# Scores of two attention branches issued in turn on two 64-row halves of the matrix array, with masks gathered behind them and more warm-up products

## The chip, the cores and the metric

The kernel runs on one core of a Trainium2 chip. The metric is device time in microseconds (us), the median of three runs. The engines that matter here are TensorE (PE for its products, PEld for the loads of its stationary operands), VectorE (DVE), ScalarE (ACT) and the queue of SyncE (SP), which issues the transfers of weights. TensorE's array has 128 rows; a product whose operands lie in 64 partitions uses one half of the rows. Products are collected in eight banks of an accumulator memory.

## The reference

Two layers of a decoder trunk on 256 tokens of 1024 channels. In each layer four token mixers read one projection of the normalised residual:

```
o_A = RG-LRU (conv4, gated linear recurrence)      o_B = GLU, causal conv31, RMSNorm, swish
o_C = (softmax1 - lambda * softmax2) V             4 heads, each with two maps of 64 query channels
o_D = softmax over the 64 keys that an indexer picks per query
      logits = relu(einsum("bqhd,bkd->bqhk", qi, ki))   8 index heads of 32 channels, one shared key
      score  = einsum("bqhk,bqh->bqk", logits, wi);  masked causally, top 64
h += W_out( sum_j sigmoid(xn W_g[j]) * (o_j W_b[j]) )
h += W_down( silu(g) * v ),  [g, v] = causal_dwconv3(RMSNorm(h) W_up)
h += sigmoid(RMSNorm(h) W_pg) * RMSNorm(p W_p)
```

Everything is float32. The change touches the score maps of o_C (differential attention) and the index logits of o_D (sparse attention).

## The kernel before

The residual is kept with channels in partitions and 256 tokens along the free axis. All weights stream once from memory in 342 pieces of at most 128 x 1024 numbers (`prep_one`, lines 213 to 215): the SP queue loads a piece, ACT rounds it to a high part `hi`, DVE subtracts to get the low part `lo`. A large product then takes three passes per 128 x 128 tile (`mm3`, lines 248 to 250: high by high, high by low, low by high), each over 256 columns. Token-major projections (lines 476 to 478) do the same with 512 columns. Five raw and six split buffers form the ring of pieces, so a piece is split when TensorE has freed an older one.

The program is written out by hand in one order. The four mixers are generators ("sides") whose steps are put between the large products by `pump`, at distances set in the table `EVERY`; a scheduler then orders each engine's own instructions. So TensorE meets a stretch of large products, then one step of a side, then large products again. The steps that the change and the prediction speak of are these:

* Index scores, in `idx_mask(b)`, line 564. For each layer, each block b of 128 queries and each group g of four index heads there is one step: 2 x 2 x 2 = 8 visits in all. The query operand holds four heads of 32 channels in 128 partitions. The key operand `ikZ` has four copies of the transposed key, copy i set to zero (by `hmask`) outside head i's 32 partitions. Four products over all 128 rows give the four maps. Kw, the number of keys, is 128 for b = 0 and 256 for b = 1.
* Differential scores, in `attend(b, hp)` of `side_c`, lines 703 and 704. For each layer, block and pair of heads there is one step, again 8 visits. Map c of a head lies in partitions 64c to 64c + 63, so each score product uses one half of the rows. Each of the four maps is followed by a mask: an identity in bf16 times the causal mask, 128 columns over all 128 rows, added into the same bank. DVE takes the maxima (line 705), ACT the exponentials.
* The sparse branch's own scores (lines 625 and 626) have the same shape, a float32 score and a bf16 mask, but with 128 channels; the change leaves them alone.

A float32 product is carried out as two passes, each with its own weight load, so it shows as two instructions in the trace. The small banks ("sp", four of them) hold all side products; the large products have four others ("mm").

At the start TensorE has no operands until ACT and DVE have split the first x tiles and weights. Line 186 gives it 12 products of a constant tile (24 passes) meanwhile.

Of the kernel before, what the change touches and what calls it, by code (L numbers as in the profile page):

```python
# [13 lines left out]
AF = mybir.ActivationFunctionType  # L14
# [4 lines left out]
P = 128  # L19
# [10 lines left out]
PIECE = 1024  # L30
EARLY = 4  # feed-forward banks computed before the mean square is known
MIX = (0, 3, 2, 1)
MIX_ORDER = (("gate", MIX[0]), ("gate", MIX[1]), ("branch", MIX[0]), ("gate", MIX[2]), ("branch", MIX[1]),
             ("gate", MIX[3]), ("branch", MIX[2]), ("branch", MIX[3]))
# how far apart the steps of the side computations lie between the products: RG-LRU, conformer,
# differential attention, sparse attention, first half of the conformer's taps
EVERY = {0: 4.8, 1: 5.1, 2: 3.3, 3: 2.9, 4: 5.5}

# columns of the channel vectors
_V = {}  # L40
# [7 lines left out]

# columns of the row vectors
_R = {}  # L50
# [6 lines left out]

# columns of the shape-only constants
_C = {}
_o = 0  # L60
for _n, _w in (("ident", 128), ("nc30", 128), ("nc38", 128), ("rope_c", 64), ("rope_s", 128), ("rope_i", 32), ("hmask", 4)):
    _C[_n] = (_o, _w)
    _o += _w
# [3 lines left out]
def unit_list(l):  # L67
    """One layer's weights in the order of their use: (key, source, pieces), a piece being
    (first k-tile, k-tiles, column ranges or counts of zero columns)."""
    u = []  # L70

    def tok(key, c0, c1, src="w_in", kt=KD):
        g = PIECE // (c1 - c0)
        u.append((key, src, [(k, g, [(c0, c1)]) for k in range(0, kt, g)]))

    def chan(key, src, c0, kt=KD, g=8):
        u.append((key, src, [(k, min(g, kt - k), [(c0, c0 + P)]) for k in range(0, kt, g)]))

    def bu(n):
        chan(("bv", n), "w_in", 1024 + n * P)  # L80
        chan(("bg", n), "w_in", 1536 + n * P)

    ple_in = [(("ple_in", i), "w_ple_in", [(0, 2, [(512 * i, 512 * i + 512)])]) for i in range(2)]
    if l:
        u.append(ple_in[0])
    for n in range(4):
        bu(n)
    if not l:
        u.append(ple_in[0])
    tok(("tok", "dq"), 3584, 4096)  # L90
    tok(("tok", "dk"), 4096, 4608)
    u.append((("ik", 0), "w_in", [(0, KD, [(4608, 4648), P - 40])]))
    tok(("tok", "cq"), 2048, 2560)
    tok(("tok", "ck"), 2560, 3072)
    tok(("tok", "cv"), 3072, 3584)
    for n in range(8):
        chan(("a", n), "w_in", n * P)
    for kind, j in MIX_ORDER:
        if kind == "gate":
            for n in range(8):  # L100
                chan(("gate", j, n), ("w_gate", j), n * P)
        else:
            for n in range(0, 8, 2):
                tok(("branch", j, n), n * P, (n + 2) * P, ("w_branch", j), 4)
    u.append(ple_in[1])
    for n in range(8):
        chan(("out", n), "w_out", n * P)
    for g in range(NG):
        chan(("upg", g), "w_up", g * P)
        chan(("upv", g), "w_up", D_FF + g * P)  # L110
    for n in range(8):
        chan(("down", n), "w_down", n * P, NG)
    for n in range(8):
        chan(("pg", n), "w_ple_gate", n * P)
    return u
# [7 lines left out]
def decoder_kernel(ctx: ExitStack, tc: tile.TileContext, w_dram, x_dram, p_dram, vec_dram, row_dram, lru_dram,  # L123
# [30 lines left out]
    def score_banks(Kw):  # L154
        """Banks for four maps [P, Kw]: (maps of the bank, bank [P, maps, Kw])."""
        n = 2 * S // Kw
        return [(range(i, i + n), smbank().rearrange("p a b -> p (a b)").rearrange("p (a b) -> p a b", a=n))
                for i in range(0, 4, n)]

# [1 line left out]
    h = [cst.tile([P, 2, S], F32, name=f"h{i}", tag=f"h{i}") for i in range(4)]  # L161
# [20 lines left out]

    # the tensor engine's clock rises with activity: keep it busy until the first operands are there
    warm = smbank()
    for _ in range(12):
        T.matmul(warm[:, 0, :], ones, ones, start=True, stop=True)

# [1 line left out]
    stream = []  # L189
# [38 lines left out]

# [1 line left out]
    def split(dst, src, scale=1.0):  # L230
        """dst = (hi, lo) from src, exactly."""
        hi, lo = dst
        if scale == 1.0:
            A.activation(hi, src, AF.Copy)  # L234
            V.tensor_tensor(lo, src, hi.bitcast(F32), op=ALU.subtract)  # L235
        else:
            A.activation(hi, src, AF.Copy, scale=scale)
            V.scalar_tensor_tensor(lo, src, scale, hi.bitcast(F32), op0=ALU.mult, op1=ALU.subtract)

    def mm3(out, wl, xs, c0, first, last):  # L240
        """out += W[:, c0:c0+128].T @ x over the piece's k-tiles."""
        wh, wlo = wl
# [23 lines left out]
    def rnorm(acc, scale, bias):  # L266
        """1 / sqrt(scale * (sum over the channels) + bias) per token: with the tokens in
        partitions [P, 2], and in every partition [P, S]."""
        t = smbank()
# [12 lines left out]
    class Norm:  # L282
        """RMSNorm over all channels of [128, 2, S] pairs. xs: split x * gain, for products whose
        result is scaled by r afterwards; xn(): split x * gain * r."""

# [50 lines left out]
    def rope(t, H, W, tab, b):  # L336
        """t [128, H, W]: rotates the first W/4 columns of each head."""
        rot = W // 4
# [17 lines left out]

    # ================= layers =================
    for l in range(L):
# [11 lines left out]

# [1 line left out]
        if l == 0:  # L372
# [32 lines left out]
        if l:  # L405
            embed(0)
# [1 line left out]
        nrm = nxt_nrm  # L408
# [20 lines left out]

# [1 line left out]
        sv = st([P, 44], "sv", 2)  # L431
# [33 lines left out]
        def tok_unit(xk, n, npieces):  # L465
            """u[:, cols] token-major, one bank per token block."""
            pcs = take(npieces)
# [15 lines left out]
        def weave(gens):  # L483
            """The steps of the generators in turn."""
            live = list(gens)
            while live:
                for g in list(live):
                    if next(g, "end") == "end":
                        live.remove(g)
                    else:  # L490
                        yield
# [13 lines left out]

# [1 line left out]
        def side_d():  # L507
# [14 lines left out]
            yield  # L522
            ikZ = st([P, 4, S], "ikZ", 1)
            qT = [bt(), bt()]
# [3 lines left out]
            def idx_key(b):  # L528
# [9 lines left out]
                T.transpose(t[:, 0, :], ikr.rearrange("p h w -> p (h w)"), ident)  # L538
                for i in range(4):
                    A.activation(ikZ[:, i, bs], t[:, 0, :], AF.Copy, scale=hmask[:, i:i + 1])  # L540
# [5 lines left out]
            def idx_mask(b):  # L546
# [13 lines left out]
                for g in range(2):  # L560
                    rl = st([P, 4, S], "e4d", 2)
                    for hs, sc in score_banks(Kw):
                        for q, i in enumerate(hs):
                            T.matmul(sc[:, q, :], iqT[:, g, :], ikZ[:, i, :Kw], start=True, stop=True)  # L564
                        A.activation(rl[:, hs[0]:hs[-1] + 1, :Kw], sc, AF.Relu)
                    for i in range(4):
# [87 lines left out]

# [1 line left out]
        def side_c():  # L656
# [36 lines left out]
            def attend(b, hp):  # L693
# [5 lines left out]
                e = st([P, 4, S], "e4", 2)  # L699
                for c, (maps, sc) in enumerate(score_banks(S)):  # L700
                    cs = slice(c * 64, (c + 1) * 64)
                    for hh in range(2):
                        T.matmul(sc[:, hh, :Kw], qT[hp][cs, hh, bs], kT[hp][cs, hh, :Kw], start=True, stop=False)  # L703
                        T.matmul(sc[:, hh, bs], ident_bf, nc30_bf, start=False, stop=True)  # L704
                    V.tensor_reduce(mx[:, 2 * c:2 * c + 2], sc[:, :, :Kw], axis=AX.X, op=ALU.max)
# [58 lines left out]

# [1 line left out]
        xa, ga = [], []  # L766
# [52 lines left out]

# [1 line left out]
        ypad = st([P, 4, S + 30], "ypad", 1)  # L821
# [66 lines left out]

# [1 line left out]
        for c in range(4):  # L890
# [33 lines left out]

# [1 line left out]
        mixed = {}  # L926
# [45 lines left out]

# [1 line left out]
        _, rs = rnorm(acc[0], 4.0 / D, eps[:, 1:2])  # L974
# [84 lines left out]
def _constants():  # L1059
# [5 lines left out]
             "rope_s": _rope_rows(128), "rope_i": _rope_rows(32),  # L1065
             "hmask": (r[:, None] // 32 == np.arange(4)[None, :]).astype(np.float32)}
    for n, a in parts.items():
# [5 lines left out]
def _chan(a):  # L1073
    """[C] or [taps, C] -> [128, C/128 * taps]: channel c*128+p at partition p."""
    a = np.asarray(a)
# [53 lines left out]
```

## Time and profile before

| | |
|---|---|
| median of 3 runs | 1068.01 us (1066.74 to 1068.23) |
| span of the profiled execution, first to last instruction | 1064.7 us |
| TensorE products, busy | 1056.7 us, 99% |
| weight loads, busy | 1018.3 us, 96% |
| VectorE, busy | 874.1 us, 82% |
| ScalarE, busy | 708.1 us, 67% |
| mean share of the DMA engines in the span (queue of weights) | 49.9% |
| mean granted TensorE clock | 0.998 |

The profiled execution's own device time is not listed apart from its span; the three timed runs lie 2.0 to 3.5 us above that span, which is what surrounds the first and last instruction. In forty slices of the span TensorE shows 8 tenths in the first and the last and 9 in every other, VectorE 9 in the second to the seventh (about 27 to 187 us, the first layer's mixers). Busy time of TensorE counts a product from its issue to its end; products overlap in the pipeline, so what one costs is read from the distance between starts.

### The profile page before, as it was taken

The page shows a single profiled execution, that of the slowest core. Times are in us where ns is not written, and L with a number is a line of the kernel's source. Part 1 is how long each engine was busy: PE and PEld are TensorE (multiplying, and loading weights), DVE is VectorE, ACT ScalarE, POOL GpSimd, SP SyncE. Part 2 cuts the span into 40 slices and gives each one's busy share as a digit, 9 for nine tenths or more (in the row PEclk, how much of TensorE's full clock was granted, in tenths as well). Part 3 has the DMA queues.
Part 4 walks back from the last instruction along what each step waited for, and adds up shares of the span by engine and source line. Part 5 has one row for each costly group of instructions (what it writes and reads, how often), then busy time and mean ns, then how long its engine had stood idle before and what let it go on. Part 6 is the DMA issues. An engine that isn't in the chain of part 4 may idle for free.

```text
span 1064.7 us, 20765 instructions
## 1 busy us (share of the span) xinstructions
PE 1056.7 (99%) x8168; PEld 1018.3 (96%) x8168; DVE 874.1 (82%) x1629; ACT 708.1 (67%) x1207; POOL 0.2 (0%) x4
## 2 busy tenths in 40 slices
PE   8999999999999999999999999999999999999998
PEld 8888999899999999999998899998999999999998
DVE  7999999868888997855787899997779789877554
ACT  7876788668466766544677769876685667665442
POOL 0000000000000000000000000000000000000000
PEclk9999999999999999999999999999999999999999
DMA  8755244434555365555554643443455554655541
GB/s 299 279 188 194 100 142 166 159 131 158 190 182 175 121 237 183 179 188 194 181 187 167 214 163 120 139 171 115 165 169 185 173 181 147 221 177 176 184 161 40
DMA packets 52369, 183.60 MB, mean 172 GB/s; under 512 B 5808, under 2 KB 6320, under 8 KB 52272
## 3 DMA queue, kind: packets, MB, share of 16 engines
q1 hardware_dynamic: 51408, 181.05, 49.9%
q8 instruction: 64, 1.05, 0.4%
q10 hardware_dynamic: 864, 1.24, 0.4%
q14 instruction: 33, 0.27, 0.1%
HBM read 181.21 MB, written 1.05 MB: 171 GB/s over the span
## 4 chain that ended last, share of the span: by engine, by line
PE 98%; DVE 1%; DMA 0%; ACT 0%; issue 0%; DVEq 0%
PE mm L249 27%; PE mm L248 27%; PE mm L250 27%; PE mm L476 3%; PE mm L478 3%; PE mm L477 3%; PE sp L703 2%; PE sp L564 1%; PE sp L625 1%; PE sp L733 1%; PE sp L704 0%; PE sp L648 0%; DMA vec<-in_vec_dram 0%; PE sp L277 0%; PE sp L271 0%; PE sp L683 0%
## 5 line engine op out<-in xcount | busy, mean ns | idle before, releaser
L248 PE MATMUL mm<-b,hi 128*128 128x256 f32 x2384 | 680.5, 286 | 1.9 <-ACT hi L214 1.7
L250 PE MATMUL mm<-b,lo 128*128 128x256 f32 x2384 | 675.6, 284 | 0.2 <-DVE lo L215 0.2
L249 PE MATMUL mm<-b,hi 128*128 128x256 f32 x2384 | 675.8, 284 | 0.0
L214 ACT ACTIVATE hi<-raw 128x1024 fp32r<-128x1024 f32 (+1 forms) x343 | 357.2, 1046 | 259.0 <-PE mm L249 199.0
L215 DVE TENSOR_TENSOR lo<-raw,hi 128x1024 fp32r<-128x1024 f32 (+1 forms) x343 | 411.1, 1204 | 122.8 <-ACT hi L214 120.1
L248 PEld LDWEIGHTS mm<-b,hi 128*128 128x128 f32 x2384 | 457.4, 192 | 3.0 <-ACT hi L214 1.9
L249 PEld LDWEIGHTS mm<-b,hi 128*128 128x128 f32 x2384 | 458.0, 192 | 1.3 <-issue 0.5
L250 PEld LDWEIGHTS mm<-b,lo 128*128 128x128 f32 x2384 | 457.8, 192 | 0.4 <-DVE lo L215 0.4
L840 DVE SCALAR_TENSOR_TENSOR b<-s,vec,b 128x256 f32<-128x256 f32 x240 | 103.6, 476 | 0.0
L476 PE MATMUL mm<-hi,b 128*128 128x512 f32 x160 | 62.9, 393 | 0.0
L478 PE MATMUL mm<-hi,b 128*128 128x512 f32 x160 | 62.5, 390 | 0.0
L477 PE MATMUL mm<-lo,b 128*128 128x512 f32 x160 | 62.4, 390 | 0.0
L1009 DVE SCALAR_TENSOR_TENSOR s<-mm,vec,s 128x255 f32<-128x255 f32 (+1 forms) x144 | 59.8, 474 | 1.7 <-ACT s L1003 1.7
L234 ACT ACTIVATE b<-b 128x512 fp32r<-128x512 f32 x56 | 35.0, 628 | 28.1 <-DVE b L1013 18.4
L235 DVE TENSOR_TENSOR b<-b,b 128x512 fp32r<-128x512 f32 x56 | 38.4, 686 | 12.3 <-ACT b L234 12.3
L478 PEld LDWEIGHTS mm<-hi,b 128*128 128x128 f32 x160 | 30.0, 188 | 6.4
L476 PEld LDWEIGHTS mm<-hi,b 128*128 128x128 f32 x160 | 30.0, 188 | 6.4
L1003 ACT ACTIVATE s<-mm,vec 128x256 f32<-128x256 f32 x72 | 36.1, 551 | 0.0
L477 PEld LDWEIGHTS mm<-lo,b 128*128 128x128 f32 x160 | 30.1, 188 | 5.8
L709 ACT ACTIVATE s<-sp,s,s 128x128 f32<-128x128 f32 (+1 forms) x32 | 16.0, 507 | 12.7 <-DVE s L706 12.7
L295 ACT ACTIVATE b<-h,vec 128x256 fp32r<-128x256 f32 x48 | 21.4, 497 | 2.4 <-DVE h L1041 2.4
L296 DVE SCALAR_TENSOR_TENSOR b<-h,vec,b 128x256 fp32r<-128x256 f32 x48 | 20.8, 478 | 0.8 <-ACT b L295 0.8
(206 smaller groups left out, 792.4 us busy)
## 6 DMA issues: line engine op xcount, KB each, us to landing
raw<-in_w_dram SPq DMA_DIRECT2D x325, 512.0 KB, 3.3
raw<-in_w_dram SPq DMA_DIRECT2D x16, 384.0 KB, 2.9
h<-in_x_dram SPq DMA_DIRECT2D x4, 256.0 KB, 5.1
b<-in_lru_dram SPq DMA_DIRECT2D x4, 256.0 KB, 6.1
out_dram<-h ACTq DMA_DIRECT2D x3, 256.0 KB, 2.5
row<-in_row_dram SPq DMA_DIRECT2D x2, 336.0 KB, 5.6
raw<-in_w_dram SPq DMA_DIRECT2D x2, 256.0 KB, 5.0
b<-in_p_dram SPq DMA_DIRECT2D x2, 256.0 KB, 4.9
```

The lines of the kernel that those rows point to most:

```text
L214: A.activation(hi[:, cs], raw[:, cs], AF.Copy)
L215: last_lo[0] = V.tensor_tensor(lo[:, cs], raw[:, cs], hi[:, cs].bitcast(F32), op=ALU.subtract).ins
L235: V.tensor_tensor(lo, src, hi.bitcast(F32), op=ALU.subtract)
L248: T.matmul(out, a, xh, start=first and k == 0, stop=False)
L249: T.matmul(out, a, xl, start=False, stop=False)
L250: T.matmul(out, b, xh, start=False, stop=last and k == nk - 1)
L476: T.matmul(outs[b], xk[k][0][:, bs], wh[:, kk, :], start=k == 0, stop=False)
L477: T.matmul(outs[b], xk[k][0][:, bs], wl[:, kk, :], start=False, stop=False)
L478: T.matmul(outs[b], xk[k][1][:, bs], wh[:, kk, :], start=False, stop=k == last)
L840: V.scalar_tensor_tensor(t, ypad[:, c, d:d + S], w[:, 31 * c + d:31 * c + d + 1], t, op0=ALU.mult, op1=ALU.add)
L1003: A.activation(cf[:, 2 * q + s_, :], bank[:, s_, :], AF.Identity, scale=w[:, 3 * c + 2:3 * c + 3], bias=bb[:, c:c + 1])
L1009: V.scalar_tensor_tensor(t, bank[:, s_, :S - d], w[:, 3 * c + 2 - d:3 * c + 3 - d], t, op0=ALU.mult, op1=ALU.add)
```

## The change

Differential scores: the two banks of a step are opened together; the four score products alternate between the two halves of the rows (c = 0, c = 1, c = 0, c = 1), each half writing its own bank; then one mask product per bank covers both maps of that bank (256 columns, the mask read twice). Only the first product of a bank clears it.

Index scores: `ikZ` and `hmask` shrink from four to two copies, even and odd 32-partition strips. A product uses 64 rows, in which one of the two heads is set to zero by the copy. The four products alternate between the halves, each half with its own bank; b = 0 now takes two banks in place of one, and ACT evaluates two relus of two maps each where b = 0 had one of four.

Warm-up: 19 products in place of 12. The rest of the diff removes comments, which shifts no instruction.

```
-    for _ in range(12):
+    for _ in range(19):
         T.matmul(warm[:, 0, :], ones, ones, start=True, stop=True)
...
-            ikZ = st([P, 4, S], "ikZ", 1)
+            ikZ = st([P, 2, S], "ikZ", 1)
...
-                for i in range(4):
+                for i in range(2):
                     A.activation(ikZ[:, i, bs], t[:, 0, :], AF.Copy, scale=hmask[:, i:i + 1])
...
-                    for hs, sc in score_banks(Kw):
-                        for q, i in enumerate(hs):
-                            T.matmul(sc[:, q, :], iqT[:, g, :], ikZ[:, i, :Kw], start=True, stop=True)
-                        A.activation(rl[:, hs[0]:hs[-1] + 1, :Kw], sc, AF.Relu)
+                    halves = score_banks(S)
+                    for v in range(2):
+                        for r, (_, sc) in enumerate(halves):
+                            rs = slice(64 * r, 64 * r + 64)
+                            T.matmul(sc[:, v, :Kw], iqT[rs, g, :], ikZ[rs, v, :Kw], start=True, stop=True)
+                    for hs, sc in halves:
+                        A.activation(rl[:, hs[0]:hs[-1] + 1, :Kw], sc[:, :, :Kw], AF.Relu)
...
-                for c, (maps, sc) in enumerate(score_banks(S)):
-                    cs = slice(c * 64, (c + 1) * 64)
-                    for hh in range(2):
-                        T.matmul(sc[:, hh, :Kw], qT[hp][cs, hh, bs], kT[hp][cs, hh, :Kw], start=True, stop=False)
-                        T.matmul(sc[:, hh, bs], ident_bf, nc30_bf, start=False, stop=True)
+                halves = score_banks(S)
+                for hh in range(2):
+                    for c, (_, sc) in enumerate(halves):
+                        cs = slice(c * 64, (c + 1) * 64)
+                        T.matmul(sc[:, hh, :Kw], qT[hp][cs, hh, bs], kT[hp][cs, hh, :Kw], start=hh == 0, stop=False)
+                for c, (maps, sc) in enumerate(halves):
+                    T.matmul(sc[:, :, bs], ident_bf, nc30_bf[:, None, :].to_broadcast([P, 2, P]), start=False, stop=True)
+                for c, (maps, sc) in enumerate(halves):
                     V.tensor_reduce(mx[:, 2 * c:2 * c + 2], sc[:, :, :Kw], axis=AX.X, op=ALU.max)
```

How the order of TensorE's instructions moves in the differential scores of the first layer, first block, first pair of heads, before (`sp` are banks, `b` the transposed keys and queries, `mask_bf` the identity and the mask):

```order
L703 MATMUL sp_2003<-b_1485,b_1483 128x128
L704 LDWEIGHTS mask_bf
L704 MATMUL sp_2003<-mask_bf 128x128
L703 MATMUL sp_2003<-b_1485,b_1483 128x128
L704 LDWEIGHTS mask_bf
L704 MATMUL sp_2003<-mask_bf 128x128
L703 MATMUL sp_2004<-b_1485,b_1483 128x128
L704 LDWEIGHTS mask_bf
L704 MATMUL sp_2004<-mask_bf 128x128
L703 MATMUL sp_2004<-b_1485,b_1483 128x128
L704 LDWEIGHTS mask_bf
L704 MATMUL sp_2004<-mask_bf 128x128
```

And the same place of TensorE now, where the lines have become 707 (score) and 709 (mask):

```order
L707 MATMUL sp_2010<-b_1492,b_1490 128x128
L707 MATMUL sp_2011<-b_1492,b_1490 128x128
L707 MATMUL sp_2010<-b_1492,b_1490 128x128
L707 MATMUL sp_2011<-b_1492,b_1490 128x128
L709 LDWEIGHTS mask_bf
L709 MATMUL sp_2010<-mask_bf 128x2x128
L709 LDWEIGHTS mask_bf
L709 MATMUL sp_2011<-mask_bf 128x2x128
```

The four masks became two of twice the width and stand behind all scores; the bank, and with it the half of the rows, changes at every score.

TensorE at the index scores of the first layer, second block, first group, before (`mm` is a large product's bank, `s` the index queries and the masked keys):

```order
L249 MATMUL mm_1211<-b_647,hi_1031 128x256
L250 MATMUL mm_1211<-b_646,lo_1032 128x256
L564 MATMUL sp_1245<-s_929,s_1149 128x256 x2
L564 MATMUL sp_1246<-s_929,s_1149 128x256 x2
L248 MATMUL mm_1211<-b_625,hi_1117 128x256
```

And now, where the line is 566 and the operands of a product are 64 partitions high:

```order
L249 MATMUL mm_1216<-b_654,hi_1034 128x256
L250 MATMUL mm_1216<-b_653,lo_1035 128x256
L566 MATMUL sp_1250<-s_936,s_1152 128x256
L566 MATMUL sp_1251<-s_936,s_1152 128x256
L566 MATMUL sp_1250<-s_936,s_1152 128x256
L566 MATMUL sp_1251<-s_936,s_1152 128x256
L248 MATMUL mm_1216<-b_632,hi_1120 128x256
```

The number of products and their neighbours stay; the banks alternate, and each product now goes to a half of the rows.

## Rows read from the trace of the kernel before

**Rows 1.** The page, busy time of each engine, share of the span, instructions:

```profile
PE 1056.7 (99%) x8168; PEld 1018.3 (96%) x8168; DVE 874.1 (82%) x1629; ACT 708.1 (67%) x1207; POOL 0.2 (0%) x4
```

**Rows 2.** Waits of PE: engine, line, waited for: us, times, longest:

```profile
PE mm L248 <- ACT hi L214: 1.7, 1, 1.7
```

**Rows 3.** Waits of ACT, same columns:

```profile
ACT hi L214 <- PE mm L249: 199.0, 156, 2.2
```

**Rows 4.** Waits of DVE, same columns:

```profile
DVE s L705 <- PE sp L704: 2.7, 8, 0.5
```

**Rows 5.** Busy by window: PE, PEld, DVE, ACT, POOL (instructions); clock, DMA, GB/s:

```profile
27.00:187.00 160.00, 160.00 (x1076) 146.57 (x1075) 154.01 (x385) 125.66 (x251) 0.00 (x0) 1.00 0.52 178
```

**Rows 6.** Timeline of PE, differential scores, 128 keys: start, us, line, operation, count:

```profile
157.39 0.28 PE L249 MATMUL mm<-b,hi 128*128 128x256 f32 x1
157.51 0.28 PE L250 MATMUL mm<-b,lo 128*128 128x256 f32 x1
157.72 0.48 PE L703 MATMUL sp<-b,b 64*128 64x128 f32 x2
158.14 0.23 PE L704 MATMUL sp<-mask_bf 128*128 128x128 bf16 x1
158.29 0.49 PE L703 MATMUL sp<-b,b 64*128 64x128 f32 x2
...
159.90 0.36 PE L248 MATMUL mm<-b,hi 128*128 128x256 f32 x1
```

**Rows 7.** Timeline of PE, differential scores, 256 keys:

```profile
198.42 0.70 PE L703 MATMUL sp<-b,b 64*128 64x256 f32 x2
199.05 0.23 PE L704 MATMUL sp<-mask_bf 128*128 128x128 bf16 x1
```

**Rows 8.** Timeline of PE, sparse scores and masks over all 128 rows:

```profile
175.22 0.44 PE L625 MATMUL sp<-s,b 128*128 128x128 f32 x2
175.49 0.22 PE L626 MATMUL sp<-s,mask_bf 128*128 128x128 bf16 x1
175.55 0.44 PE L625 MATMUL sp<-s,b 128*128 128x128 f32 x2
```

**Rows 9.** Timeline of PE, index scores, 256 keys:

```profile
104.95 1.89 PE L564 MATMUL sp<-s,s 128*128 128x256 f32 x8
106.49 0.47 PE L248 MATMUL mm<-b,hi 128*128 128x256 f32 x1
106.80 0.28 PE L249 MATMUL mm<-b,hi 128*128 128x256 f32 x1
```

**Rows 10.** Timeline of PE, a transposition of 40 partitions between large products:

```profile
62.17 0.39 PE L477 MATMUL mm<-lo,b 128*128 128x512 f32 x1
62.40 0.39 PE L478 MATMUL mm<-hi,b 128*128 128x512 f32 x1
62.72 0.25 PE L907 MATMUL sp<-con,s 40*128 40x40 f32 x1
62.90 0.50 PE L476 MATMUL mm<-hi,b 128*128 128x512 f32 x1
63.23 0.40 PE L477 MATMUL mm<-lo,b 128*128 128x512 f32 x1
```

**Rows 11.** Busy by window at the start; columns as in rows 5:

```profile
1.04:5.28 4.24, 4.24 (x20) 4.24 (x21) 0.10 (x1) 1.28 (x1) 0.00 (x0) 1.00 0.73 196
5.28:8.70 3.42, 1.49 (x10) 1.09 (x10) 3.06 (x10) 3.35 (x9) 0.00 (x0) 1.00 1.04 392
8.70:12.10 3.40, 3.40 (x18) 3.40 (x18) 3.12 (x9) 3.02 (x7) 0.00 (x0) 0.50 1.04 408
```

**Rows 12.** Timelines of PE and DVE at the start:

```profile
1.04 4.96 PE L186 MATMUL sp<-ones 128*128 128x128 f32 x24 [1.04 <-DVE ones L166]
11.26 1.23 DVE L215 TENSOR_TENSOR lo<-raw,hi 128x1024 fp32r<-128x1024 f32 x1 [0.21 <-ACT hi L214]
12.90 0.28 PE L250 MATMUL mm<-b,lo 128*128 128x256 f32 x1
```

More of the change, by code (lines that the diff above doesn't have):

```diff
@@ L60 @@
 _o = 0
-for _n, _w in (("ident", 128), ("nc30", 128), ("nc38", 128), ("rope_c", 64), ("rope_s", 128), ("rope_i", 32), ("hmask", 4)):
+for _n, _w in (("ident", 128), ("nc30", 128), ("nc38", 128), ("rope_c", 64), ("rope_s", 128), ("rope_i", 32), ("hmask", 2)):
     _C[_n] = (_o, _w)
@@ L1065, in _constants @@
              "rope_s": _rope_rows(128), "rope_i": _rope_rows(32),
-             "hmask": (r[:, None] // 32 == np.arange(4)[None, :]).astype(np.float32)}
+             "hmask": (r[:, None] // 32 % 2 == np.arange(2)[None, :]).astype(np.float32)}
     for n, a in parts.items():
```

## The prediction

> **What bounds the kernel now.** I read the page first: TensorE is busy in 99% of the span [rows 1]. Busy can still mean waiting, so the waits come next. Apart from the warm-up's own start, TensorE waits once worth naming, 1.7 us for the first split weights [rows 2]; ScalarE waits 199 us in 156 pieces for TensorE to free a split buffer [rows 3], so weights lie ready before they are wanted. The end is therefore set by the sum of TensorE's slots, and a slot saved anywhere behind the start is saved at the end, as long as VectorE keeps up. The tightest place for that is the first layer's mixers, where VectorE is busy 154 of 160 us [rows 5].
>
> Then I looked at slots, by distances between starts. Large products stand 0.12 us apart (157.39, 157.51). The first score on a half of the rows starts 0.21 us behind the last one, and a map costs 0.57 to 0.58 us from score to score (157.72, 158.29) [rows 6]. At 256 keys its two passes last 0.63 us to the mask instead of 0.42 [rows 6, 7]; the difference of 0.21 is 2 x 128 more columns, so 128 columns stream in 0.105 us. A map of 128 keys is then 0.21 us of score columns and 0.06 of mask (175.49 to 175.55 in rows 8), 0.27 in all, and 0.31 us of its 0.58 is something else. The sparse branch has the same two products over all 128 rows and takes 0.33 us a map [rows 8]. What differs is the change between 64 and 128 rows, there and back. Of the 0.31, about 0.09 is emptying at entry (0.21 against 0.12), about 0.11 the load of the first weights, which nothing covers, and 0.10 emptying at exit.
>
> The Trainium skill (TensorEngine Tiling (Array Packing), Key Properties) says that a change of tiling mode, not of tile, drains TensorE. These rows agree, 0.31 us for the round trip. By the same sentence a turn from one half to the other should cost nothing, which no row here shows.
>
> **The change part by part.** *Differential scores.* Each of the 8 visits made four round trips, one for each map, and now makes one: 3 x 0.31 = 0.93 us a visit, 8 x 0.93 = 7.4 us less. The masks stream as many columns as before, 2 x 256 for 4 x 128: nothing. That counts score passes as still coming one after another, as the two of one map do.
>
> *Index scores.* These ran over all 128 rows and paid no round trip: eight passes of 256 columns took 1.54 us, and the next large product kept 0.31 instead of 0.12, in all 1.73 us or 0.216 a pass, with loads hidden [rows 9]. Eight visits now each pay one: 0.09 emptying, 0.11 first load, then 0.10 emptying and 0.10 for the next large product's load. The last two are read at a transposition of 40 partitions: it starts 0.32 us behind a product where 0.23 is usual, holds 0.18 us for what is 0.03 us of columns by the 0.105 above and a short load, and the next product keeps 0.33 for 0.23 [rows 10]. In all 0.40 us a visit, 3.2 us more. The nearest rows bound it by 0.31 and 0.40 a visit, 2.5 to 3.2; I take the upper, since a large product's load follows, not a short mask's.
>
> *Two halves at once.* No row shows a product on one half next to one on the other: a mask always lay between. The bounds: a turn of halves hides nothing, or every second pass disappears behind its neighbour. Two passes of one map share a half and stay in order, so what can overlap is the second pass of one map with the first of the next. There are three such turns in a visit. At 128 keys a pass streams 0.105 us and its load takes about as long (0.11), so if loads come one after another nothing is gained. At 256 keys a pass streams 0.21. If the other half's weights are loaded only when the last pass before has begun, as a load stands one pass ahead now, 0.105 of it overlaps: 3 x 0.105 = 0.32 us a visit, with four differential and four index visits of 256 keys 2.5 us. If they are loaded earlier, 0.21 overlaps at each turn: 0.63 us a visit, 5.0 us. If the two halves also load at the same time, 128 keys gain 0.32 us a visit as well, 2.5 us more. I take the first, 2.5 us, which asks only for what the rows already show of loads, between 0 and 7.6.
>
> The Trainium skill (TensorE: Matmul & The Clock Gate, Part 3) says that products in distinct row groups start about 4 ns apart and run side by side, 3.07 times as fast with four tiles at 512 columns. No run here shows it; by it the gain would be nearer to 5.0 or 7.6 than to 2.5. It is the second rival below.
>
> *Warm-up.* The 24 passes run from 1.04 to 6.00 us, and the first 20 take 4.24 us, 0.21 each, twice the 0.105 of the rest of the kernel: the lower level, 1.2 GHz. Then TensorE idles 1.7 us for its operands; in 5.28 to 8.70 it is busy 1.49 of 3.42 us, and behind that stretch the granted clock is 0.50 from 8.70 to 12.10 [rows 2, 11, 12]. Fourteen more passes at 0.105 end at about 7.5 us, before the first operands (7.7). With the idle gap mostly filled I expect the higher level, 2.4 GHz, to stay. But the stretch is 18 products at twice their time, 1.7 us at most, and the second weight piece limits what of it can be had: its low part is ready at 11.26 + 1.23 = 12.49 us, and TensorE uses it at 12.90 [rows 12]. So 0.4 us, and a wait for VectorE takes the place of the slow clock. Bounds: 0 and 0.4; below nothing if that new wait of about 1 us lets the clock fall once more, 1.7 us lost, which I hold unlikely since it is shorter than the gap before and lies between full stretches.
>
> *Other engines.* ScalarE loses 8 key copies and gains 4 small relus; it is 67% busy [rows 1] and ahead by the buffers it waits for: nothing. VectorE's first maximum of a differential visit now waits for both halves and the masks. In its queue behind it stand splits of weights and the conformer's taps. It waited 2.7 us in 8 such places [rows 4]; the second maximum now waits for nothing, so I cost the exchange at nothing. The cover is the weights split ahead; without it, at most the 0.9 us that the visit shrinks would be handed back once.
>
> The sum against the span of 1064.7 us: -7.4 + 3.2 - 2.5 - 0.4 = -7.1, a span of 1057.6. The median of the runs lies 3.3 us above that span; carried along, 1068.0 - 7.1 = 1060.9 us.
>
> **The rivals.** *The halves do not overlap.* Scores merely stand one after another, and index scores only lose: -7.4 + 3.2 - 0.4 = -4.6, 1063.4 us. For it: nothing in the trace has ever overlapped two products' columns. Against: the halves hold separate weights and banks.
>
> *They overlap fully.* At 256 keys -9.6, 1058.4 us; with loads side by side as well -12.1, 1055.9 us. For it: nothing shared is visible in the rows but the order of issue; against: loads have always stood one pass ahead.
>
> *A turn between halves empties the array.* Then each of three turns a visit costs 0.09 to empty and 0.11 for an uncovered load, 0.20. Differential visits save only 3 x (0.31 - 0.20) = 0.33, 2.6 us in all; index visits pay 0.40 + 0.60 = 1.0, 8.0 us: -2.6 + 8.0 - 0.4 = +5.0, 1073.0 us, slower. It decides from a turn price x of 0.10: 24 x (0.31 - x) and 0.4 are gained and 3.2 + 24x lost, which is even there. For it: the one kind of turn that the rows have is this dear. Against: that turn changes the number of rows, which a turn of halves does not.
>
> *VectorE becomes the bound.* It has 6 us of slack in 27 to 187 us [rows 5], and the visits of 128 keys lie there. If it gave their 2 x 0.93 us back in each layer, -3.4, 1064.5 us. Against: rows 3.
>
> **How the numbers follow.** Forecast 1060.9: 0.33. No overlap 0.24, full overlap 0.21 with loads in turn and 0.08 with loads side by side, emptying turns 0.09, VectorE 0.05. The range runs from 1056.5, which leaves out the loads side by side, to 1065.0, which leaves out the emptying turns: 17 in 100 are outside. A measurement of this kernel tells about 0.2%, 2.1 us, from no change; all cases but the emptying turns lie below 1065.9. I leave 0.06 for within 0.2%, since waits I cost at nothing could eat the rest of the smallest gains: faster 0.85, same 0.06, slower 0.09.
>
> **What would show it.** In the profile of the changed kernel a differential visit of 128 keys should last about 2.18 - 0.93 = 1.25 us from first score to next large product, and one of 256 keys 8 x 0.105 more, about 2.1, without overlap, 1.8 with one load ahead, 1.5 with full overlap. An index visit of 128 keys should be 0.4 us dearer than before, one of 256 keys 0.1 dearer. Starts of passes on different halves closer than 0.1 us would show overlap; a gap of 0.2 us at each change of bank would show emptying. At the start, the clock should stay at 1.00 behind 8.7 us, with a wait for the second piece's low part. The prediction is wrong if index visits come out faster by the round trip's price or more, if turns are dear, or if TensorE shows waits of more than 1 us in 90 to 215 us.

## The result, and the profile after

| | before | changed |
|---|---|---|
| median, us | 1067.38 (1066.51 to 1068.23, 4 runs) | 1053.05 (1052.97 to 1053.19, 4 runs) |
| span of the profiled execution, us | 1064.7 | 1051.3 |
| TensorE products busy, us | 1056.7 | 1043.2 |

The ratio of the times is 0.9865, with a 95% interval of 0.9851 to 0.9879: 14.3 us faster, where 7.1 was forecast and 1056.5 was the lower end of the range. The direction was right; the forecast gain was half of the measured one, and the time lies below the range.

The page of the changed kernel, busy time by engine as in [rows 1], and the waits of PE, with [rows 2] as their counterpart:

```profile
PE 1043.2 (99%) x8166; PEld 1008.4 (96%) x8166; DVE 872.7 (83%) x1629; ACT 704.2 (67%) x1203; POOL 0.2 (0%) x4
...
PE sp L186 <- DVE ones L166: 1.0, 1, 1.0
PE mm L250 <- DVE lo L215: 1.0, 2, 0.8
PE sp L610 <- DVE b L348: 0.6, 2, 0.3
PE mm L248 <- ACT hi L214: 0.5, 2, 0.3
```

TensorE is still busy for 99% of the span. Of its waits the one at line 610 is new: the transposition of the sparse branch's key waits for VectorE's rotation. VectorE has also entered the chain of work that ended last; its shares by engine before, and then in the changed kernel:

```profile
PE 98%; DVE 1%; DMA 0%; ACT 0%; issue 0%; DVEq 0%
...
PE 89%; DVE 8%; issue 1%; DMA 1%; ACT 0%; SPq 0%; DVEq 0%
```

The first differential visit of the changed kernel on PE (start, us, line, operation, count; 128 keys), to be laid beside [rows 6], and then one of 256 keys, beside [rows 7]; the last row is where that visit ended before:

```profile
156.67 0.28 PE L250 MATMUL mm<-b,lo 128*128 128x256 f32 x1
156.88 0.72 PE L707 MATMUL sp<-b,b 64*128 64x128 f32 x8
157.53 0.39 PE L709 MATMUL sp<-mask_bf 128*128 128x256 bf16 x2
157.67 0.37 PE L248 MATMUL mm<-b,hi 128*128 128x256 f32 x1
...
195.43 1.14 PE L707 MATMUL sp<-b,b 64*128 64x256 f32 x8
196.50 0.39 PE L709 MATMUL sp<-mask_bf 128*128 128x256 bf16 x2
196.64 0.36 PE L248 MATMUL mm<-b,hi 128*128 128x256 f32 x1
...
201.45 0.36 PE L248 MATMUL mm<-b,hi 128*128 128x256 f32 x1
```

From first score to next large product a visit takes 0.79 us at 128 keys (2.18 before) and 1.21 at 256 (3.03 before, 198.42 to 201.45). Look at the eight passes of 256 keys alone: 1.07 us from the first start to the first mask, where eight passes of 256 columns one behind another are 8 x 0.21 = 1.68 us. So they do not run one behind another. The same visit cut off at 156.89 us, PE and then PEld:

```profile
156.88 0.38 PE L707 MATMUL sp<-b,b 64*128 64x128 f32 x2
...
156.88 0.19 PEld L707 LDWEIGHTS sp<-b,b 64*128 64x128 f32 x2
```

Two passes begin at the same 156.88 and are over in 0.38 us together, and two weight loads take 0.19 us, the length of one. Both the loads and the passes of two products run side by side.

The index visit of 256 keys, beside [rows 9]:

```profile
105.17 1.13 PE L566 MATMUL sp<-s,s 64*128 64x256 f32 x8
106.23 0.39 PE L248 MATMUL mm<-b,hi 128*128 128x256 f32 x1
106.46 0.28 PE L249 MATMUL mm<-b,hi 128*128 128x256 f32 x1
```

It took 1.54 us to the next large product and now takes 1.06, although it enters and leaves 64 rows. The one of 128 keys, before and then now, takes 0.64 us for 0.81, and entry and exit take most of that back:

```profile
101.19 1.05 PE L564 MATMUL sp<-s,s 128*128 128x128 f32 x8
102.00 0.36 PE L248 MATMUL mm<-b,hi 128*128 128x256 f32 x1
...
101.46 0.72 PE L566 MATMUL sp<-s,s 64*128 64x128 f32 x8
102.10 0.39 PE L248 MATMUL mm<-b,hi 128*128 128x256 f32 x1
```

The start of the changed kernel by window (PE, PEld, DVE, ACT, POOL busy; clock, DMA, GB/s), beside [rows 11], and the two rows that set the start, DVE and PE, beside [rows 12]:

```profile
5.28:8.70 3.42, 2.98 (x24) 2.58 (x23) 3.12 (x9) 2.96 (x8) 0.00 (x0) 1.00 1.01 386
8.70:12.10 3.40, 2.99 (x23) 2.57 (x21) 2.80 (x9) 3.00 (x7) 0.00 (x0) 1.00 1.04 414
...
11.45 1.23 DVE L215 TENSOR_TENSOR lo<-raw,hi 128x1024 fp32r<-128x1024 f32 x1 [0.34 <-ACT hi L214]
12.73 0.39 PE L250 MATMUL mm<-b,lo 128*128 128x256 f32 x1 [0.76 <-DVE lo L215]
```

TensorE is busy in 2.98 of 3.42 us instead of 1.49, and the clock stays at 1.00 from 8.70 to 12.10, where it was 0.50. The second piece's low part ends at 12.68 and is used at 12.73; before it was used at 12.90.

Where the 13.4 us between the two spans went, by the change of distance between the same large products in both traces: differential visits -1.39 and -1.24 (128 keys), -1.82 twice (256 keys) in the first layer, -12.5 in both; index visits -0.07 at 128 keys and -0.46 at 256, -2.1 in all; the wait at line 610 with the load behind it +0.48 in each layer, +1.0; the start +0.2. The medians differ by 0.9 us more than the spans: the runs of before lie up to 1.7 us apart, those of the changed kernel 0.2. Wherever a run's time and span are both listed, they are 1.7 to 2.0 us apart. So the profiled execution of before was one of the shorter ones, and the 2.0 to 3.5 us that were taken for what surrounds its instructions are in part this spread, as are the 3.3 us that the prediction carried along.

### The profile page after: what moved, and what is told of

Its sections match the earlier page's. It is cut to its first block, busy times and chain, and to the rows that moved or that the text cites. A ratio compares the mean times of both kernels' runs of the same rounds, so it can differ in the third digit from the quotient of the medians.

```text
span 1051.3 us, 20757 instructions
## 1 busy us (share of the span) xinstructions
PE 1043.2 (99%) x8166; PEld 1008.4 (96%) x8166; DVE 872.7 (83%) x1629; ACT 704.2 (67%) x1203; POOL 0.2 (0%) x4
## 3 DMA queue, kind: packets, MB, share of 16 engines
q10 hardware_dynamic: 864, 1.24, 0.3%
## 4 chain that ended last, share of the span: by engine, by line
PE 89%; DVE 8%; issue 1%; DMA 1%; ACT 0%; SPq 0%; DVEq 0%
PE mm L248 25%; PE mm L249 25%; PE mm L250 25%; PE mm L476 3%; PE mm L478 3%; PE mm L477 3%; DVE lo L215 2%; DVE b L846 1%; DVE s L582 1%; DMA raw<-in_w_dram 1%; PE sp L628 1%; PE sp L739 1%; PE sp L651 0%; DVE s L581 0%; DVE s L575 0%
## 5 line engine op out<-in xcount | busy, mean ns | idle before, releaser
L715 ACT ACTIVATE s<-sp,s,s 128x128 f32<-128x128 f32 (+1 forms) x32 | 15.9, 509 | 17.5 <-DVE s L712 17.5
```

## The experiments

Theory A: the two halves of the rows work as two arrays, with their own loads, passes and order. Theory B: they take turns, with no more overlap than the forecast gave them. The others were put up as the runs came in. Runs of the kernel before were repeated in each set; ratios are against those. Their medians lie between 1066.7 and 1067.5 us, so between runs of different sets the times alone do not decide a difference of less than about 0.7 us.

**Differential scores alone** (`e1_diff`), on the kernel before (the edit in words; it is the change's own part):

```
-  score, mask, score, mask on one half; then on the other
+  scores in turn on the two halves, then one mask per bank
```

> Only the differential scores are changed. Theory A (the two halves work as two arrays: load and both passes of a product on one half run beside those on the other, so a pair of products costs what one does): the visits keep the 1.17 to 1.39 us (128 keys) and 1.82 us (256 keys) that they lost in the changed kernel's trace, 12.2 us in all, less up to 1.0 us if the new wait for the sparse key's transposition comes back; 11.2 to 12.2 us faster than the kernel before. Theory B (halves only take turns, as the forecast had it, and the index scores and warm-up bring the rest): 7.4 to 9.9 us faster.

1053.91 us against 1067.0, ratio 0.9875 (0.9861 to 0.9888), 13.1 us: more than A's 12.2, out of B's reach. All four visits of 128 keys lost 1.39 us here, and the wait at line 610 does not occur; spans differ by 13.0, of which eight visits are 12.8.

**Index scores alone** (`e2_index`), on the kernel before:

```
-  T.matmul(sc[:, q, :], iqT[:, g, :], ikZ[:, i, :Kw], ...)
+  T.matmul(sc[:, v, :Kw], iqT[rs, g, :], ikZ[rs, v, :Kw], ...)
```

Before, a product uses 128 rows and one of four zeroed copies; now it uses 64 rows in turn and one of two. The rest of the edit is the change's own and left out here.

> Only the index scores are changed. Theory A: 0.40 us more for entering and leaving 64 rows a visit, 0.45 less for columns at 128 keys and 0.87 less at 256 keys, so 4 x 0.05 + 4 x 0.46 = 2.1 us faster (1.5 to 2.5). Theory B: 0.7 to 3.2 us slower.

1065.54 us, ratio 0.9987 (0.9978 to 0.9996): 1.5 us faster, so A's sign, at the lower end of its range. Its trace has exactly the changed kernel's steps, -0.07 and -0.46 a visit, -2.1 us behind the start; its start happened to be 1.0 us longer, with the clock at the lower level up to about 14 us.

**Warm-up alone** (`e3_warm`), on the kernel before: `range(12)` became `range(19)`.

> Only the warm-up is longer, 19 products for 12. Theory C: the four runs of the kernel before lie 1.7 us apart, those of the changed kernel 0.2, because the stretch at the lower clock falls differently from run to run before and does not come at all after; then the clock stays at 1.00 and the median falls by 0.5 to 1.0 us while the lowest run stays where it was. Rival D: the start waits for split weights either way (the changed kernel's trace is 0.07 us ahead at the third weight piece and 0.17 behind at 23.5 us); then 0.0 within 0.2 us, and the spread of the runs stays.

1067.08 us, ratio 1.0001 (0.9993 to 1.0010), runs from 1066.6 to 1068.4: nearest to D. The interval, -0.7 to +1.1 us, does not shut out the lower part of C's gain. The trace shows no gain at all: the low clock is gone from the start, and a wait has come in its place:

```profile
8.70:12.10 3.40, 3.14 (x24) 2.73 (x23) 2.96 (x9) 2.83 (x6) 0.00 (x0) 1.00 1.04 411
...
12.72 0.39 PE L250 MATMUL mm<-b,lo 128*128 128x256 f32 x1 [0.76 <-DVE lo L215]
```

The first row is the window that was at 0.50 before. In the second TensorE waits 0.76 us for the low part and starts at 12.72, near the 12.90 of before; at 23.5 us it is 0.2 us behind the trace of before. What makes the runs of before differ by up to 1.7 us is thus not what the warm-up mends; it stays open.

**Both maps on one half** (`e4_one_half`), on the changed kernel:

```
-                        cs = slice(c * 64, (c + 1) * 64)
+                        cs = slice(0, 64)
```

> The changed kernel, but both maps of a head are computed from the operands of map 0, in partitions 0 to 63, so no product can run beside another; banks, order and masks stay (map 1's values are therefore wrong). Theory A: a visit of 128 keys takes 1.25 to 1.30 us from first score to next large product in place of 0.80, one of 256 keys 2.1 in place of 1.21; 4 x 0.45 + 4 x 0.87 = 5.3 us slower than the changed kernel, 9 us faster than the one before. Theory B: the same time as the changed kernel within 0.5 us.

1057.01 us, ratio 0.9904 (0.9889 to 0.9919): 4.0 us slower than the changed kernel. The visits of 128 and 256 keys on PE:

```profile
156.84 1.16 PE L707 MATMUL sp<-b,b 64*128 64x128 f32 x8
157.93 0.39 PE L709 MATMUL sp<-mask_bf 128*128 128x256 bf16 x2
158.07 0.37 PE L248 MATMUL mm<-b,hi 128*128 128x256 f32 x1
...
195.64 1.99 PE L707 MATMUL sp<-b,b 64*128 64x256 f32 x8
197.57 0.39 PE L709 MATMUL sp<-mask_bf 128*128 128x256 bf16 x2
197.72 0.37 PE L248 MATMUL mm<-b,hi 128*128 128x256 f32 x1
```

This is the forecast's case without overlap, and its visits are the forecast's: 1.23 us (1.25) and 2.08 (2.1). Order, banks and masks are those of the changed kernel, so it is the second half of the rows that makes passes run side by side, 0.44 and 0.86 us a visit. The other 0.95 us that each visit lost came with the gathered masks, and so with three changes of the number of rows fewer, there and back. The run is 1.3 us less slow than A's 5.3 because TensorE comes later and other engines are in time: the wait at line 610 is gone, 1.0 us, and so is a late start of the second differential visit, 0.4 us.

**Half by half** (`e5_grouped`), on the changed kernel:

```
-                for hh in range(2):
-                    for c, (_, sc) in enumerate(halves):
+                for c, (_, sc) in enumerate(halves):
+                    for hh in range(2):
```

> The changed kernel with the four differential scores issued half by half (both products of the lower half, then both of the upper); banks, masks and all else stay. Theory A1 (products are handed to their halves in program order, so one that waits for its half holds up those behind it): only the last product of the lower half runs beside the first of the upper, three product times a visit in place of two: 0.22 us more at 128 keys, 0.43 at 256, 2.6 us slower than the changed kernel. Theory A2 (each half draws its own products ahead of the order): the same time within 0.3 us. Theory B (only neighbours' second and first pass overlap): 0.11 and 0.21 us less overlap at two of three turns, at most 1 us slower.

1053.05 us, the changed kernel's time: A2. The first visit on PE, whole and cut off at 157.06 us:

```profile
157.04 0.72 PE L707 MATMUL sp<-b,b 64*128 64x128 f32 x8
157.69 0.39 PE L709 MATMUL sp<-mask_bf 128*128 128x256 bf16 x2
...
157.04 0.39 PE L707 MATMUL sp<-b,b 64*128 64x128 f32 x2
```

Two passes still begin at 157.04, where passes on one half stand 0.11 us apart (`e4_one_half`). So the upper half's first pass begins with the lower half's first, although the second pass of that product and a whole further product of the lower half stand between them in the program. Alternating the order is not what brings the overlap. What is left of the edit is that no mask stands between the scores; no run has the two halves in turn with masks between.

**Index scores on quarters** (`e6_quarters`), on the changed kernel (the edit cut to the lines of its products):

```
+                    banks = [smbank() ... for _ in range(4)]
+                    for i, sc in enumerate(banks):
+                        rs = slice(32 * i, 32 * i + 32)
+                        T.matmul(sc[:, :Kw], iqT[rs, g, :], ikZ[rs, :Kw], start=True, stop=True)
```

> The changed kernel with the index scores on four quarters of 32 rows, one head, one bank and one product each; no zeroed copies of the keys (8 fewer copies on ScalarE, 16 more relus). Theory A, carried on to four arrays: one product time a visit in place of two, 0.21 us less at 128 keys and 0.42 at 256, 8 visits, 2.5 us of TensorE's slots. Theory V (VectorE is the bound from 100 to 187 us, where it is busy 47.00 of the last 47 us): of these 2.5 us nearly all comes back as waits for VectorE before 187 us in each layer, and the time falls by 0 to 0.6 us. Rival: quarters share what loads weights, and the visit loses nothing.

1056.63 us, 3.6 slower than the changed kernel. An index visit of 256 keys on PE, and the second differential visit, behind it by 60 us:

```profile
104.97 0.71 PE L564 MATMUL sp<-s,s 32*128 32x256 f32 x8
105.61 0.39 PE L248 MATMUL mm<-b,hi 128*128 128x256 f32 x1
...
164.79 0.53 PE L705 MATMUL sp<-b,b 64*128 64x128 f32 x2 [1.71 <-DVE b L814]
165.67 1.22 PE L705 MATMUL sp<-b,b 64*128 64x128 f32 x6 [0.35 <-ACT s L713]
```

Four quarters do work as four arrays: 0.64 us to the next large product, against 1.06 and 1.54, as A said. But the saved 1.27 us of the first layer, and more, are waited for at the second differential visit. Its two banks are those of the first visit, which ScalarE's exponentials (L713) empty behind VectorE's maxima. In the second layer that visit costs 1.43 us more, about what was saved. In the first it costs 3.1 us more, because the exponentials are late there too: they begin at 163.76 us, in the changed kernel at 162.39. ScalarE's work is late by that much from a weight split on, which had waited 1.16 us for its transfer. That split, and then TensorE by window, in the same trace:

```profile
152.52 1.06 ACT L214 ACTIVATE hi<-raw 128x1024 fp32r<-128x1024 f32 x1 [1.16 <-DMA raw<-in_w_dram]
...
162.00:164.00 2.00, 1.09 (x10) 0.85 (x8) 2.00 (x4) 1.99 (x4) 0.00 (x0) 1.00 0.39 158
...
167.10:170.50 3.40, 3.40 (x18) 3.40 (x17) 3.40 (x13) 2.07 (x5) 0.00 (x0) 0.50 0.23 46
```

TensorE is idle for almost half of 162 to 164 us while VectorE and ScalarE are full, and behind that the clock falls to 0.50, where large products stand 0.21 us apart instead of 0.12: some 2.1 us more. None of the theories had a slower kernel. Theory V was right that the saving is waited for, but the wait is for banks that ScalarE empties, and it is longer than the saving.

**Taps of the conformer later** (`e8_taps_later`) and the same with quarters (`e9_quarters_taps`):

```
-EVERY = {0: 4.8, 1: 5.1, 2: 3.3, 3: 2.9, 4: 5.5}
+EVERY = {0: 4.8, 1: 5.8, 2: 3.3, 3: 2.9, 4: 6.2}
```

> The changed kernel with the conformer's taps set further apart (5.8 and 6.2 for 5.1 and 5.5), which takes about 5 of VectorE's 46 taps out of 100 to 187 us in each layer and puts them behind. Theory V: the waits for the transposition of the sparse branch's key (0.48 us in each layer with its uncovered load) go, and the time falls by 0.9 to 1.3 us. Rival: the taps then fall due at the branch product near 250 us and TensorE waits there; the same time or slower.

> Both of the last two edits, quarters and later taps. Theory V: with VectorE relieved the 2.5 us of slots reach the end, 3.4 to 3.8 us faster than the changed kernel. Rival: as much as the quarters save is waited for elsewhere, 0.9 to 1.5 us faster.

1070.36 us (ratio 1.0034, 1.0021 to 1.0047) and 1071.47 us (1.0048, 1.0031 to 1.0065): both slower than before. That is the rival of the first edit; for the second, both theories missed, since both had it faster than the changed kernel. Waits of PE in `e8_taps_later`:

```profile
PE mm L248 <- ACT b L234: 6.2, 2, 3.1
PE sp L277 <- DVE s L274: 6.1, 2, 3.0
```

The wait at line 610 is gone, and the norm behind the taps (L274) is late at its branch product instead, 3 us in each layer and 3 more for what follows. In all the gap between large products there grows by 7.8 and 8.2 us in the two layers. From 277.4 to 284.2 us the clock is 0.50, with TensorE busy in 4.28 of the 7.40 us before; that costs another 1.6 us behind the gap, and 2.6 in the second layer.

**Taps a little later** (`e10_taps_little`): 5.25 and 5.7.

> The changed kernel with the conformer's taps set a little further apart (5.25 and 5.7 for 5.1 and 5.5), which takes 1 to 2 of VectorE's 46 taps, 0.5 to 1.0 us, out of 100 to 187 us in each layer without reaching the branch product that they are due at. Theory V: the wait at line 610 goes or halves, 0.5 to 1.0 us faster. Rival: they still fall due, 1 us or more slower.

1054.79 us, 1.7 slower than the changed kernel: the rival's time, but not its reason, since TensorE does not wait at the branch product (L277). The second differential visit now waits for its bank as well (L707 on ACT L715, 0.6 us in all) and line 610 waits 0.9. What the taps leave free on VectorE goes into a wait for a weight piece's high part, 1.3 us where the changed kernel has 0.3 in 100 to 140 us:

```profile
102.06 1.23 DVE L215 TENSOR_TENSOR lo<-raw,hi 128x1024 fp32r<-128x1024 f32 x1 [1.30 <-ACT hi L214]
```

**Warm-up of 12 in the changed kernel** (`e7_warm12`): `range(19)` back to `range(12)`.

> The changed kernel with the 12 warm-up products of before. Theory D (the start waits for split weights, so the longer warm-up brings nothing): the same time within 0.3 us, perhaps with a wider spread of the runs. Rival: the forecast's 0.4 us or more, since the stretch at the lower clock comes back.

1053.10 us, the same; runs from 1052.6 to 1053.6. D holds here too: the clock is 0.68 in 8.70 to 12.10, and the second piece's low part is used at 12.50.

**Four small operations a layer to ScalarE** (`e11_to_act`), on the changed kernel:

```
-                            V.tensor_scalar(sa, rl[:, i, :Kw], w, None, op0=ALU.mult)
+                            A.activation(sa, rl[:, i, :Kw], AF.Copy, scale=w)
...
-                V.tensor_copy(ikr, ik[b][:, None, 0:32].to_broadcast([P, 4, 32]))
+                A.activation(ikr, ik[b][:, None, 0:32].to_broadcast([P, 4, 32]), AF.Copy)
```

> The changed kernel with six small operations a layer (the first weighting of the index maps, 0.31 to 0.41 us each, and the fourfold copy of the index key) on ScalarE in place of VectorE: about 1.0 us less for VectorE in each layer before 115 us, out of the stage in which it is the bound. Theory V: the wait at line 610 goes in both layers, 0.5 to 1.0 us faster than the changed kernel. Rival: the wait hangs on the order of VectorE's queue just before it, not on its total; the same time within 0.2 us.

1052.10 us (1051.99 to 1052.32), ratio 0.9857 (0.9840 to 0.9873): 0.95 us faster than the changed kernel, and the fastest version here. Its interval against before overlaps the changed kernel's, but its runs all lie below those of `e7_warm12` in the same set (1052.6 to 1053.6). Both edited lines run twice a layer, so it is four operations a layer and not six: VectorE has 8 instructions fewer in all (1629 to 1621) and is busy 1.9 us less. All the waits of PE that its trace lists, and the last step of the key's rotation on VectorE, in the changed kernel and then here:

```profile
PE sp L186 <- DVE ones L166: 1.0, 1, 1.0
PE mm L250 <- DVE lo L215: 1.0, 2, 0.8
...
168.60 0.19 DVE L348 TENSOR_TENSOR b<-s,s 128x32 f32<-128x32 f32 x1
...
167.95 0.20 DVE L348 TENSOR_TENSOR b<-s,s 128x32 f32<-128x32 f32 x1
```

The wait at line 610 is gone in both layers. In the 4 us before the rotation ends VectorE has the same operations in the same order in both traces, 0.65 us earlier here. So it was the amount of work ahead of the rotation, as theory V had it, and not the order just before it.

## Why the prediction was right or wrong

*What bounds the kernel*: right. TensorE's slots set the end, and each slot saved shows in the sum until VectorE, or a bank that ScalarE has not emptied, holds it up.

*Differential scores, fewer round trips*: right. 7.4 us forecast; `e4_one_half` gives 0.95 us a visit, 7.6 us. Whether all of it is the change of the number of rows is not shown: by the prediction's own rows a map of the sparse branch pays 0.06 of the 0.31 us as well (0.33 us against 0.27 of columns), and there that number does not change.

*Index scores, round trip of 0.40 us a visit*: right. A visit lost 0.07 us at 128 keys and 0.46 at 256, and 0.44 and 0.86 of overlap, taken over from the differential visits, stand against the 0.40. Starts of single passes in the changed kernel's trace give 0.38 to 0.39 for entry, first load, exit and the next load together.

*Two halves at once*: this is the step that failed. I took 2.5 us, bounded at 7.6; it is 10.4: 0.44 us in each of eight visits of 128 keys and 0.86 in each of eight of 256. Even the rival with loads side by side, 1055.9 us, lies above the 1053.05 measured, and the prediction's own sign of being wrong came true: index visits of 256 keys are faster by more than the round trip's price. Two premises were wrong. "Two passes of one map share a half and stay in order, so what can overlap is the second pass of one map with the first of the next" held the halves to the program's order: only three turns in a visit could overlap, by half a pass or a whole one. The trace after and `e5_grouped` show that each half draws its own work, so every pass has a partner, four pairs for eight passes. And at 128 keys "if loads come one after another nothing is gained" was taken to hold: the loads run side by side. The upper bound, meant to hold any overlap, was built on the same order and so was no bound. A plain one was at hand: half of the streaming, 16 visits with 8 x 0.105 or 8 x 0.21, which is 10.1 us. With the 0.112 and 0.216 us by which passes on one half stand apart in `e4_one_half` it is 10.5, so nearly all that could vanish did.

The sentence of the Trainium skill (TensorE: Matmul & The Clock Gate, Part 3) that products in distinct row groups run side by side, starting 4 ns apart, agrees with the pairs here, which start at the same 156.88 us. I had set it against "loads have always stood one pass ahead", which was seen only of loads for the same rows; the trace before had no row on two halves, and the page should have weighed more. The Trainium skill (TensorEngine Tiling (Array Packing), Key Properties) has a change of mode drain TensorE and not one of tile. The pairs agree, and the rival of the emptying turns was wrong.

*Warm-up*: 0.4 us forecast; the medians of `e3_warm` and `e7_warm12` differ by 0.1 us or less from those of the same kernel with the other warm-up, though runs of one kernel spread by 1 us and more, so 0.4 is not excluded by the times alone. The wait for the second piece's low part was foreseen and took the place of the slow clock, as written; that it ends at 12.5 to 12.7 us in every version makes the gain smaller still. (The 1.00 that [rows 11] prints for 1.04 to 5.28 us does not contradict the lower level there: the trace records a granted clock from 5.28 us on only, and the passes before that stand 0.21 us apart, those behind it 0.11.)

*Other engines, costed at nothing*: wrong by 1.3 us of the span. Line 610 waits 0.29 us in each layer and costs 0.48 with its load; the second differential visit starts its upper half 0.16 us late, for the bank. The rival of VectorE came true in small, in the stage that it named, where VectorE is busy throughout (47.00 of 47 us before, too); the wait and the chain's share of VectorE in the changed kernel, and `e11_to_act`, show it:

```profile
140.00:187.00 47.00, 46.71 (x384) 45.10 (x383) 47.00 (x123) 39.09 (x94) 0.00 (x0) 1.00 0.47 155
...
168.94 0.30 PE L610 MATMUL sp<-con,b 128*128 128x128 f32 x1 [0.29 <-DVE b L348]
```

[rows 3] argued against it and spoke of weights alone; the late operand was a side's. (The rival's time follows as 1064.6 from its own -3.4; 1064.5 is a slip.)

Sum: -7.6 + 3.1 - 10.4 + 1.3 + 0.2 = -13.4 us, the difference of the spans. The overlap alone put the forecast 7.9 us off; that the other engines and the start came out 1.9 us dearer than forecast hid part of it, by luck.

## What to carry to other kernels

Here products that use half of the rows streamed in half the time when products of the other half, with their own bank, stood near them and nothing that uses all rows stood between; the order among them made no difference (`e5_grouped`). Gather what needs all rows behind them: three changes of the number of rows fewer a visit, there and back, brought 0.95 us together with the masks that were merged. Bound an unseen overlap by the work that could vanish, not by a guess at the order of issue; and when the first engine gives up time, look at the side chains' operands and banks too, not only at the weights.

## What the runs showed of the hardware

A pass on the second half starts ahead of products that stand before it in the program (`e5_grouped`, both halves' first passes at 157.04 us). On one half alone all loads but the first stay hidden (`e4_one_half`: eight passes of 128 columns and their first load in 1.09 us to the mask). Float32 products on four quarters of 32 rows take 0.64 us where all rows take 1.54 (`e6_quarters`, 256 keys). The granted clock, in the same run, was 0.50 from 165.1 us on, behind a stretch in which TensorE was busy 1.09 of 2.00 us and stood idle 1.71 us at once.
